# An encoder layer on one core: input also loaded by columns, and the latents turned behind the first Fourier product

## The chip, the core and the metric

The kernel runs on one core of a Trainium2 chip. The core has a matrix engine (TensorE, PE in the profile, with its weight loads as PEld), a vector engine (VectorE, DVE), an activation engine (ScalarE, ACT), a general engine (GpSimd, POOL) and a queue engine (SyncE, SP) that mostly issues DMA transfers. POOL can issue transfers too. Each engine works through its instructions in a fixed order and waits on semaphores for the others. [...]

The metric is the time of one execution on the device in microseconds (us), the median of several runs.

## The reference, cut to what matters

Two sequences of 1024 rows and 1024 columns go through one layer. Both changed stages lie at its start: the normalised and modulated input `h`, its projection to the latents (`q_lat`, `kv_lat`, `k_pe`), and the Fourier mixing of the remaining columns.

```python
def layer(x, c, ...):
    mod = jax.nn.silu(c) @ w_ada + b_ada
    sh1, sc1, ga1, sh2, sc2, ga2 = [m[:, None, :] for m in jnp.split(mod, N_MOD, axis=-1)]
    h = rmsnorm(x, g_mix) * (1.0 + sc1) + sh1
    z = h @ w_in
    q_lat, kv_lat, k_pe, f_in = z[..., :o1], z[..., o1:o2], z[..., o2:o3], z[..., o3:]
    y_mla = mla_group(q_lat, kv_lat, k_pe, g_q_lat, w_uq, g_kv_lat, w_ukv)
    y_four = fourier_group(f_in, w_four)      # 2-D Fourier transform, real part, by groups
    mix = jnp.concatenate([y_mla, y_four], axis=-1) @ w_out
    x = x + ga1 * mix
    h2 = rmsnorm(x, g_ffn) * (1.0 + sc2) + sh2
    ffn = (jax.nn.silu(h2 @ w_gate) * (h2 @ w_up)) @ w_down
    return x + ga2 * ffn
```

`rmsnorm` scales each row by the inverse root of its mean square. After the layer comes a last `rmsnorm`. All is float32.

## The kernel before, in words

Products of float32 are made from two halves: `split` puts a rounded high part (`hh`, `eoh`, `lh`, `wz_h`, ...) on ScalarE and the rest (`hl`, `eol`, `ll`, `wz_l`, ...) on VectorE (line 62 and 63), and `mm3` multiplies high with high, high with low and low with high (lines 78 to 80).

The first stage works on eight **pairs**, numbered 0 to 7: four for each sequence, each of two tiles of 128 rows. For pair k:

- `x_load(k)` loads the two row tiles `xt` (512 KB each; lines 353 to 356), from a ring of four buffers, two pairs' worth.
- `norm(k)` takes their mean squares on ScalarE (line 366), turns them into the row factors `rs_r` in six small steps on POOL (`rstd`, lines 103 to 110) and scales the rows on VectorE (line 369).
- `flip(k, g)`, for g from 0 to 3, transposes two of the eight column blocks of both tiles on TensorE (line 382: 4 transposes of 128x128, 16 in a pair), modulates them on ScalarE out of PSUM into `hf` (line 389) and splits `hf` into `hh` and `hl`. `hf` has one buffer, `hh` and `hl` two.
- `evenodd(k, i)` adds (i = 0) or subtracts (i = 1) the two tiles on POOL (line 400) and splits the result into `eoh`, `eol`.
- `zproj(k, u)` is the projection to the latents for tile u, 24 matmuls with 448 columns. Behind it come the mean squares of the latents on ScalarE (lines 413, 414), `rstd` on POOL, the scaling into `lat` on VectorE (lines 425, 426) and the store of the keys, `ckv_d`.
- `latents(k, u)` transposes `lat` on TensorE (line 440, four transposes) and splits and stores it (`lat_d`).
- `fourier_in(k, i)` is the Fourier product of the sum or the difference, 24 matmuls with 280 or 256 columns.

`pair(k)` puts these in order: TensorE does the projection of pair k and, between its products, the transposes of pair k+1, so that the next pair's `hh` is there when pair k ends. A generator (`extras`) is stepped between the products. In pair 0 it makes the eight products with folded output weights (`fold_out`, line 251; each leaves PSUM through VectorE into `so`, line 253, and is stored), in pairs 1 to 3 the eight chunks of a product with `w_ada` (line 216; 1 MB each, two buffers), in pairs 4 and 5 the products of line 311. `lat`, `so` and a few others share a ring of three buffers. Ahead of pair 0 stand the loads and products of the first modulation and the weights of the Fourier product.

The order on each engine is set when the program is built: the calls are laid out in the order of the code, shifted by a scheduler's estimate of when each can start. `behind()` and `tc.issue_after(...)` place work behind an instruction named before. A transfer waits in its queue until its buffer is free, and whatever stands behind it in that queue waits too.

Of the kernel before, what the change touches and what calls it, by code (L numbers as in the profile page):

```python
# [12 lines left out]
F32 = mybir.dt.float32  # L13
# [3 lines left out]
ALU = mybir.AluOpType  # L17
# [35 lines left out]
def hybrid_encoder_kernel(ctx: ExitStack, tc: tile.TileContext, a: dict):  # L53
# [109 lines left out]
    with ExitStack() as st:  # L163
# [5 lines left out]
        def bank():  # L169
            return pp.tile([P, 512], F32, tag="b", name="bank")  # L170

        def xtile():
            return w2.tile([P, D], F32, tag="x", name="xt", bufs=4)
# [178 lines left out]
        def x_load(k):  # L352
            s, j = pairs[k]
            st1["x", k] = [xtile() for _ in range(2)]
            for u in range(2):
                nc.sync.dma_start(st1["x", k][u], xs[s][rows(j, u), :])

        def norm(k):
            if ("x", k) not in st1:
                x_load(k)  # L360
            ms = tiny.tile([P, 2], F32, name="ms")
            xt = st1["x", k]
            for u in range(2):
                t = xt[u]
                jk = w.tile([P, D], BF16, tag="junk", name="junk", bufs=1)
                nc.scalar.activation(jk, t, AF.Square, scale=1.0 / 32.0, accum_out=ms[:, u : u + 1])
            r = rstd(ms, 2)
            for u in range(2):
                nc.vector.tensor_scalar(out=xt[u], in0=xt[u], scalar1=r[:, u : u + 1], scalar2=None, op0=ALU.mult)

        def flip(k, g):
            s, j = pairs[k]
            if g == 0:
                st1["hf", k] = w2.tile([P, NC, 2, P], F32, tag="hf", name="hf", bufs=1)
                st1["hh", k] = w.tile([P, NC, 2, P], F32R, tag=f"hh{k % 2}", name="hh")
                st1["hl", k] = w.tile([P, NC, 2, P], F32R, tag=f"hl{k % 2}", name="hl")
            hf, xt = st1["hf", k], st1["x", k]
            pt = bank().rearrange("p (c u t) -> p c u t", c=2, u=2)
            for c in range(2):
                for u in range(2):  # L380
                    cc = 2 * g + c
                    nc.tensor.transpose(pt[:, c, u, :], xt[u][:, cc * P : (cc + 1) * P], ident)
# [96 lines left out]
        def wide(tag, shape=(P, 4, 512)):  # L479
            return (w2 if tag == "hf" else w).tile(list(shape), F32, tag=tag, name="wide")  # L480
# [41 lines left out]
        x_load(1)  # L522
# [4 lines left out]
        wo2 = wo_load(0, wada_tile().rearrange("p a b -> p (a b)").rearrange("p (a b) -> p a b", a=2))  # L527
        mod_mm(0, 6, ch[6])
# [10 lines left out]
        with behind():  # L539
            fold_pe(wpe, gq)  # L540
        zproj(0, 0)
        norm(1)
        evenodd(0, 1)
        nk = len(pairs)
        more = extras()

        def pair(k, also=None):
            if k + 2 < nk:
                x_load(k + 2)
            if also is not None:  # L550
                also(0)
            if k > 0:
                zproj(k, 0)
# [22 lines left out]
            if k > 0:  # L576
                if k == nk - 1:
                    latents(k, 0)
                latents(k, 1)
# [4 lines left out]
            if k == 0:  # L584
                latents(k, 1)
# [3 lines left out]
        for k in range(nk - 1):  # L589
            pair(k)  # L590
# [1171 lines left out]
def _layout(i):  # L1762
# [10 lines left out]
    for s in range(2):  # L1773
# [4 lines left out]
        "x0": sq["x_prompt"][slots], "x1": sq["x_sample"][slots],  # L1778
        "cT": c.reshape(2, NC, P).transpose(2, 1, 0),
# [31 lines left out]
```

## Time and profile before

| | us |
|---|---|
| median of 3 runs | 2044.28 (2043.81 to 2044.97) |
| the profiled execution | 2045.76 |
| its span | 2043.9 |
| up to the end of pair 0's projections | 59.5 |
| from there to the first projection of pair 1 | 22.2 |
| pairs 1 to 6 | 131.7 |
| pair 7 | 17.6 |
| the rest of the layer | 1812.9 |

In the profile, a row of a timeline gives start, length, engine, line of the kernel, operation, output and inputs, and the number of instructions merged; in brackets stands the idle time of the engine before it and what ended it. A row of waits gives engine and line, what it waited for, the total in us, how often, and the longest. A row of groups gives busy us and mean ns of one, then the idle time before them. Matmuls overlap: their cost on the path is the distance from one start to the next, not their length.

### The profile page before, as it was taken

The numbers are of one execution on the slowest core, as the hardware profiler recorded it, in microseconds if no ns is written. First come the engines' busy times: TensorE is split into PE (matmuls) and PEld (weight loads), VectorE is DVE, ScalarE is ACT, GpSimd is POOL, SyncE is SP. The second block draws the span as 40 slices with busy tenths as digits, with TensorE's granted clock in tenths as the row PEclk, the third lists the DMA queues.
The fourth block names the chain that finished last, engine by engine and source line by source line (L and its number), as shares of the span: only waits on it lengthen the run. The fifth ranks groups of instructions, "written<-read, shape, count | busy, mean of one in ns | idle before, by whom it ended". The sixth has DMA issues, their size and how long they took to land.

```text
span 2043.9 us, 27849 instructions
## 1 busy us (share of the span) xinstructions
PE 1986.5 (97%) x9610; PEld 1613.6 (79%) x9610; DVE 1415.6 (69%) x2082; ACT 897.3 (44%) x1741; POOL 832.3 (41%) x1021
## 2 busy tenths in 40 slices
PE   6999999999999999999999999999999999999997
PEld 3788877888787777888888888877788888888876
DVE  3667757766677668878777676777766656667684
ACT  3656635555465554333333365453233333336451
POOL 0555213111313317879779410332654454420142
PEclk8999999999999999999999999999999999999999
DMA  9785694544644375546555587674333232258672
GB/s 363 229 258 180 220 336 132 129 104 106 158 114 129 119 277 192 195 157 210 194 166 196 173 306 251 216 233 140 129 118 103 97 110 103 96 187 276 226 228 89
DMA packets 183817, 370.30 MB, mean 181 GB/s; under 512 B 19004, under 2 KB 60476, under 8 KB 180604
## 3 DMA queue, kind: packets, MB, share of 16 engines
q1 hardware_dynamic: 165004, 310.72, 45.8%
q0 software_dynamic: 18672, 57.81, 9.5%
q8 instruction: 75, 1.23, 0.3%
q14 instruction: 66, 0.54, 0.1%
HBM read 256.46 MB, written 120.39 MB: 184 GB/s over the span
## 4 chain that ended last, share of the span: by engine, by line
PE 52%; DVE 3%; DMA 3%; POOL 1%; issue 1%; ACT 1%; SPq 0%; DVEq 0%; ACTq 0%; POOLq 0%
PE bank L78 17%; PE bank L79 17%; PE bank L80 17%; DVE wl L63 1%; DMA draw<-s_d 1%; ACT wh L62 1%; DMA val<-x_d 1%; DVE val L138 1%; POOL val L138 1%; DMA draw<-t_d 0%; DMA rgu<-in_wgu_dram 0%; DVE val L1610 0%; POOL rs_y L106 0%; DMA draw<-in_w_down_dram 0%; SPq L1570 0%
## 5 line engine op out<-in xcount | busy, mean ns | idle before, releaser
L78 PE MATMUL bank<-H,wh 128*128 128x512 f32 x1224 | 477.8, 390 | 6.9 <-DVE val L138 5.8
L80 PE MATMUL bank<-H,wl 128*128 128x512 f32 x1224 | 476.6, 390 | 0.2 <-DVE wl L63 0.2
L79 PE MATMUL bank<-H,wh 128*128 128x512 f32 x1224 | 476.3, 389 | 0.0
L138 DVE TENSOR_TENSOR val<-bank,val 128x512 f32<-128x512 f32 x244 | 166.7, 688 | 166.9 <-PE bank L80 165.8
L78 PEld LDWEIGHTS bank<-H,wh 128*128 128x128 f32 x1224 | 229.8, 188 | 59.0 <-DVE val L138 8.3
L80 PEld LDWEIGHTS bank<-H,wl 128*128 128x128 f32 x1224 | 229.8, 188 | 50.4 <-DVE wl L63 2.3
L79 PEld LDWEIGHTS bank<-H,wh 128*128 128x128 f32 x1224 | 229.8, 188 | 47.1
L63 DVE TENSOR_TENSOR wl<-draw,wh 128x512 fp32r<-128x512 f32 x286 | 202.2, 740 | 86.3 <-ACT wh L62 85.7
L62 ACT CAST wh<-draw 128x512 fp32r<-128x512 f32 x286 | 169.0, 620 | 158.6 <-PE bank L79 81.6
L79 PE MATMUL bank<-wl,wh 128*128 128x512 f32 x572 | 223.7, 391 | 2.8 <-DVE wl L63 2.8
L138 POOL TENSOR_TENSOR val<-val 128x512 f32<-128x512 f32 x58 | 83.4, 1445 | 343.4 <-DVE val L1584 189.6
L80 PE MATMUL bank<-wh,wl 128*128 128x512 f32 x572 | 222.7, 389 | 0.0
L78 PE MATMUL bank<-wh 128*128 128x512 f32 x572 | 222.6, 389 | 0.0
L62 ACT CAST wh<-rgu 128x512 fp32r<-128x512 f32 x171 | 106.3, 623 | 253.6 <-PE bank L79 192.1
L63 DVE TENSOR_TENSOR wl<-val,wh 128x512 fp32r<-128x512 f32 x133 | 139.7, 1052 | 68.8 <-ACT wh L62 68.7
L63 DVE TENSOR_TENSOR wl<-rgu,wh 128x512 fp32r<-128x512 f32 x171 | 169.1, 989 | 9.7 <-ACT wh L62 9.6
L62 ACT CAST wh<-val 128x512 fp32r<-128x512 f32 x133 | 82.3, 622 | 179.1 <-PE bank L79 156.5
L135 POOL TENSOR_TENSOR val<-rgu 128x512 f32<-128x512 f32 x80 | 114.8, 1435 | 99.2 <-DMA rgu<-in_wgu_dram 95.5
L79 PEld LDWEIGHTS bank<-wl,wh 128*128 128x128 f32 x572 | 107.4, 188 | 28.5 <-DVE wl L63 6.3
L78 PEld LDWEIGHTS bank<-wh 128*128 128x128 f32 x572 | 107.4, 188 | 22.5 <-ACT wh L62 0.2
L80 PEld LDWEIGHTS bank<-wh,wl 128*128 128x128 f32 x572 | 107.4, 188 | 21.9
L135 POOL TENSOR_TENSOR val<-val 128x512 f32<-128x512 f32 x89 | 119.3, 1357 | 1.3
(383 smaller groups left out, 3908.1 us busy)
## 6 DMA issues: line engine op xcount, KB each, us to landing
rgu<-in_wgu_dram SPq DMA_DIRECT2D x86, 512.0 KB
draw<-s_d SPq DMA_DIRECT2D x143, 256.0 KB
s_d<-val POOLq DMA_DIRECT2D x88, 256.0 KB, 3.8
draw<-t_d SPq DMA_DIRECT2D x88, 256.0 KB
s_d<-val SPq DMA_DIRECT2D x66, 256.0 KB
draw<-in_w_down_dram SPq DMA_DIRECT2D x55, 256.0 KB
wada<-in_w_ada_dram SPq DMA_DIRECT2D x13, 1024.0 KB
xt<-in_x_dram SPq DMA_DIRECT2D x16, 512.0 KB
```

What stands on the lines that cost most here:

```text
L62: here["a"] = nc.scalar.copy(hi, src).ins
L63: here["v"] = nc.vector.tensor_tensor(out=lo, in0=src, in1=rd(hi), op=ALU.subtract).ins
L78: nc.tensor.matmul(out, lh, rh, start=first, stop=False, skip_group_check=cont)
L79: nc.tensor.matmul(out, lh, rl, start=False, stop=False, skip_group_check=cont)
L80: nc.tensor.matmul(out, ll, rh, start=False, stop=last, skip_group_check=cont)
L135: return eng.tensor_tensor(out=out, in0=x, in1=y, op=ALU.subtract).ins
L138: return eng.tensor_tensor(out=out, in0=x, in1=y, op=ALU.add).ins
```

## The change

The input lies in DRAM a second time, turned by the host's layout: `xT0` and `xT1`, one block of 128x2048 for each pair, with the columns of x on the partitions. For pairs 1 to 7 the kernel loads this block straight into `hf` (`xT_load`), on SP's queue for pairs 1 and 2 and on POOL's queue for pairs 3 to 7. The transposes of x and the scaling of its rows are left out for these pairs. Since the row factors now run along the free dimension, two transposes turn them into PSUM (`scale_cols`), and two products on VectorE multiply `hf` by them in place; ScalarE modulates `hf` in place. The row tiles are still loaded, for their mean squares alone. `hf` has two buffers now and `xt` two instead of four.

The order is changed, too. `x_load(1)` and `xT_load(1)` come behind three weight loads, `norm(1)` ahead of pair 0's projections, pair 0 has an order of its own (`first_pair`), with its first Fourier product right behind its projections, and both latents of a pair are turned behind its first Fourier product.

```diff
         def xtile():
-            return w2.tile([P, D], F32, tag="x", name="xt", bufs=4)
+            return w2.tile([P, D], F32, tag="x", name="xt", bufs=2)
...
+        def xT_load(k):
+            s, j = pairs[k]
+            st1["hf", k] = w2.tile([P, NC, 2, P], F32, tag="hf", name="hf", bufs=2)
+            (nc.gpsimd if k > 2 else nc.sync).dma_start(st1["hf", k], a[f"xT{s}"][j])
...
             r = rstd(ms, 2)
+            if k > 0:
+                st1["r", k] = r
+                return
             for u in range(2):
                 nc.vector.tensor_scalar(out=xt[u], in0=xt[u], scalar1=r[:, u : u + 1], scalar2=None, op0=ALU.mult)
+
+        def scale_cols(k):
+            hf, r = st1["hf", k], st1.pop(("r", k))
+            pr = bank()[:, :256].rearrange("p (u t) -> p u t", u=2)
+            for u in range(2):
+                nc.tensor.transpose(pr[:, u, :], r[:, u : u + 1].broadcast_to([P, P]), ident)
+            for g in range(2):
+                gs = slice(4 * g, 4 * g + 4)
+                nc.vector.tensor_tensor(out=hf[:, gs], in0=hf[:, gs], in1=pr.unsqueeze(1).broadcast_to([P, 4, 2, P]), op=ALU.mult)
...
-            pt = bank().rearrange("p (c u t) -> p c u t", c=2, u=2)
-            for c in range(2):
-                for u in range(2):
-                    cc = 2 * g + c
-                    nc.tensor.transpose(pt[:, c, u, :], xt[u][:, cc * P : (cc + 1) * P], ident)
+            if k > 0:
+                pt = hf[:, 2 * g : 2 * g + 2]
+            else:
+                pt = bank().rearrange("p (c u t) -> p c u t", c=2, u=2)
+                for c in range(2):
+                    for u in range(2):
+                        cc = 2 * g + c
+                        nc.tensor.transpose(pt[:, c, u, :], xt[u][:, cc * P : (cc + 1) * P], ident)
...
-        x_load(1)
         wpe = w.tile([P, 2, HEADS * ROPE], F32, tag="lh", name="wpe", bufs=2)
...
         wo2 = wo_load(0, wada_tile().rearrange("p a b -> p (a b)").rearrange("p (a b) -> p a b", a=2))
+        x_load(1)
+        xT_load(1)
...
+        with behind():
+            norm(1)
+        placed = here["p"]
         zproj(0, 0)
-        norm(1)
-        evenodd(0, 1)
+        with tc.issue_after(placed):
+            evenodd(0, 1)
...
+        def first_pair():
+            x_load(2)
+            xT_load(2)
+            next(more)
+            zproj(0, 1)
+            fourier_in(0, 0)
+            scale_cols(1)
+            for g in range(4):
+                flip(1, g)
+            norm(2)
+            latents(0, 0)
+            for h in range(2):
+                fold_out(h, wo2, wuvT, gq)
+            next(more)
+            evenodd(1, 0)
+            next(more)
+            fourier_in(0, 1)
+            latents(0, 1)
+            evenodd(1, 1)
 
         def pair(k, also=None):
             if k + 2 < nk:
                 x_load(k + 2)
+                xT_load(k + 2)
...
-            if 0 < k < nk - 1:
+            if k < nk - 1:
+                scale_cols(k + 1)
                 flip(k + 1, 0)
                 flip(k + 1, 1)
             next(more, None)
             zproj(k, 1)
-            if k == 0:
-                fold_out(0, wo2, wuvT, gq)
-                flip(k + 1, 0)
-                flip(k + 1, 1)
-                fold_out(1, wo2, wuvT, gq)
-            if k < nk - 1:
-                latents(k, 0)
...
             fourier_in(k, 0)
-            if k > 0:
-                if k == nk - 1:
-                    latents(k, 0)
-                latents(k, 1)
+            latents(k, 0)
+            latents(k, 1)
...
-        for k in range(nk - 1):
+        first_pair()
+        for k in range(1, nk - 1):
             pair(k)
```

TensorE behind pair 0's second projection, before (`xt` is pair 1's x, `wuvT` the folded weights, `lat` pair 0's latents, `eoh` its sum of tiles):

```order
L80 MATMUL bank<-wz_h,hl 128x448
L251 MATMUL bank<-wada,wuvT 128x512 x2
L382 MATMUL bank<-ident,xt 128x128 x2
L251 MATMUL bank<-wada,wuvT 128x512
L382 MATMUL bank<-ident,xt 128x128 x6
L251 MATMUL bank<-wada,wuvT 128x512
L440 MATMUL bank<-ident,lat 128x128 x4
L382 MATMUL bank<-ident,xt 128x128 x8
L251 MATMUL bank<-wada,wuvT 128x512 x2
L78 MATMUL bank<-wcs_h,eoh 128x280
```

And now, from the end of the first Fourier product, which starts right behind the projections (`rs_r` holds pair 1's row factors):

```order
L80 MATMUL bank<-wcs_h,eol 128x280
L383 MATMUL bank<-ident,rs_r 128x128 x2
L461 MATMUL bank<-ident,lat 128x128 x4
L251 MATMUL bank<-wada,wuvT 128x512 x8
L78 MATMUL bank<-wcs_h,eoh 128x256
```

The 16 transposes of x are gone, and the latent's four now stand ahead of all eight folded products.

VectorE in the same place, before, from the last step of the key rotation of pair 0's second tile:

```order
L422 TENSOR_TENSOR t_562<-bank,ropes 128x32
L425 TENSOR_SCALAR lat<-bank,rs_r 128x256
L426 TENSOR_SCALAR lat<-bank,rs_r 128x128
L253 TENSOR_SCALAR so<-bank,gq 128x512
L63 TENSOR_TENSOR kv<-lat,kv 128x128
L369 TENSOR_SCALAR xt<-xt,rs_r 128x1024
L253 TENSOR_SCALAR so<-bank,gq 128x512
L63 TENSOR_TENSOR hl<-hf,hh 128x512
```

And now:

```order
L443 TENSOR_TENSOR t_564<-bank,ropes 128x32
L446 TENSOR_SCALAR lat<-bank,rs_r 128x256
L447 TENSOR_SCALAR lat<-bank,rs_r 128x128
L63 TENSOR_TENSOR kv<-lat,kv 128x128
L386 TENSOR_TENSOR hf<-hf,bank 128x1024 x2
L63 TENSOR_TENSOR ll<-bank,lh 128x512
L253 TENSOR_SCALAR so<-bank,gq 128x512
L63 TENSOR_TENSOR hl<-hf,hh 128x512
```

The two products that scale pair 1's columns stand behind the second latent, and the first eviction of a folded product behind them.

SP's queue around the loads of pair 1, before (`ckv_d` is the store of pair 0's keys):

```order
L356 DMA xt<-in_x_dram 128x1024 x2
L524 DMA wpe<-in_wpe_dram 128x512
L526 DMA wuvT<-in_wuvT_dram 128x512
L244 DMA wada<-in_w_out_dram 128x2x1024
L356 DMA xt<-in_x_dram 128x1024 x2
L244 DMA wada<-in_w_out_dram 128x2x1024
L260 DMA wq_d<-wq 128x1536
```

And now:

```order
L546 DMA wpe<-in_wpe_dram 128x512
L548 DMA wuvT<-in_wuvT_dram 128x512
L244 DMA wada<-in_w_out_dram 128x2x1024
L356 DMA xt<-in_x_dram 128x1024 x2
L361 DMA hf<-in_xT_dram 128x2048
L244 DMA wada<-in_w_out_dram 128x2x1024
L264 DMA w_1504<-in_w_dram 128x512
L356 DMA xt<-in_x_dram 128x1024
L260 DMA wq_d<-wq 128x1536
L356 DMA xt<-in_x_dram 128x1024
L452 DMA ckv_d_96<-kv 128x128
L452 DMA ckv_d_97<-kv 128x128
```

Pair 1's loads stand where pair 2's stood, and pair 2's two row tiles come one by one behind them.

More of the change, by code (lines that the diff above doesn't have):

```diff
@@ L479, in wide @@
         def wide(tag, shape=(P, 4, 512)):
-            return (w2 if tag == "hf" else w).tile(list(shape), F32, tag=tag, name="wide")
+            if tag == "hf":
+                return w2.tile(list(shape), F32, tag=tag, name="wide", bufs=2)
+            return w.tile(list(shape), F32, tag=tag, name="wide")
         cols0 = [(0, 2048)]
@@ L1778, in _layout @@
         "x0": sq["x_prompt"][slots], "x1": sq["x_sample"][slots],
+        **{f"xT{s}": x[slots].reshape(2, 4, P, NC, P).transpose(1, 4, 3, 0, 2)
+           for s, x in enumerate((sq["x_prompt"], sq["x_sample"]))},
         "cT": c.reshape(2, NC, P).transpose(2, 1, 0),
```

8 lines of the change are left out of this document (3 added, 5 removed).

## The prediction, made before the changed kernel was run

> **What bounds the kernel now.** I read the page's first part, then the span cut into stages, then TensorE's waits in the stage that the change touches, then the order of time there. (Columns of the stages: length, then busy us of each engine with its instructions, granted clock, share of the DMA engines, GB/s.)
>
> ```profile
> PE 1986.5 (97%) x9610; PEld 1613.6 (79%) x9610; DVE 1415.6 (69%) x2082; ACT 897.3 (44%) x1741; POOL 832.3 (41%) x1021
> ...
> 0.00:59.50 59.50, 40.27 (x213) 26.99 (x214) 28.11 (x67) 21.17 (x52) 9.65 (x20) 0.89 0.88 337
> 59.50:81.70 22.20, 17.74 (x89) 12.46 (x88) 14.66 (x30) 13.13 (x31) 13.72 (x32) 0.85 0.57 179
> 81.70:213.40 131.70, 130.45 (x842) 110.27 (x841) 88.17 (x184) 78.96 (x195) 68.15 (x149) 1.00 0.70 222
> 213.40:231.00 17.60, 16.66 (x107) 15.86 (x106) 12.10 (x29) 9.54 (x27) 7.14 (x18) 1.00 0.49 141
> 231.00:2043.90 1812.90, 1781.36 (x8368) 1448.00 (x8366) 1272.53 (x1775) 774.54 (x1439) 733.68 (x804) 1.00 0.54 174
> ```
> ```profile
> PE bank L382 <- DVE xt L369: 4.5, 1, 4.5
> PE bank L440 <- DVE lat L425: 2.2, 3, 0.9
> ```
>
> TensorE is the bound. The change touches the first two rows' end and the next two: 59.5 to 81.7 us is the first pair (weights' preparation before it), 81.7 to 213.4 are pairs 1 to 6, then pair 7. In pairs 1 to 6 TensorE is busy 130.45 of 131.70 us, so a TensorE instruction taken out there is worth its whole time. In the first pair it is idle 4.5 us. The order behind 231 us is the same in both kernels, row for row, so I move that stage as it is. The profiled execution took 2045.76 us, 1.86 around its span of 2043.9; the median of the three runs is 2044.28, 1.48 lower. I sum against the profile and take the difference over to the median.
>
> **The transposes taken out.** In a pair, 16 transposes of the next pair's x (L382) stand in two groups of 8:
>
> ```profile
> 86.55 1.03 PE L382 MATMUL bank<-ident,xt 128*128 128x128 f32 x8
> 87.52 1.06 PE L216 MATMUL bank<-wada,scT 128*32 128x512 f32 x8
> ...
> 93.45 0.60 PE L440 MATMUL bank<-ident,lat 128*128 128x128 f32 x4
> 93.89 1.04 PE L382 MATMUL bank<-ident,xt 128*128 128x128 f32 x8
> 94.86 1.06 PE L216 MATMUL bank<-wada,scT 128*32 128x512 f32 x8
> 95.85 0.39 PE L78 MATMUL bank<-wcs_h,eoh 128*128 128x280 f32 x1
> 99.06 0.60 PE L440 MATMUL bank<-ident,lat 128*128 128x128 f32 x4
> ```
> ```profile
> 206.18 1.04 PE L382 MATMUL bank<-ident,xt 128*128 128x128 f32 x8
> 206.97 0.38 PE L78 MATMUL bank<-wcs_h,eoh 128*128 128x280 f32 x1
> ```
>
> From start to next start a group takes 0.97 us ahead of other small work and 0.79 ahead of a long product. Of the twelve groups in pairs 1 to 6, eight are of the first kind and four of the second: 8 x 0.97 + 4 x 0.79 = 10.9 us. In their place come two transposes of the row scale in each pair. Four transposes take 0.44 (93.45 to 93.89), so two take about 0.25, 1.5 in six pairs. Net 9.4 us earlier. That is the firmest term.
>
> **What takes their place on the other engines.** VectorE loses two scalings of x (0.75 each) and gains two products of hf with a PSUM operand of 128x1024. The nearest rows are 128x512 with a PSUM operand: 0.68. Doubling gives at most 1.36, and one fixed part less gives some 1.23. So VectorE has about 1 us more in a pair, on 88.17/131.70, 67% busy; that hides behind TensorE. ScalarE runs the same eight activations, now from SBUF. No row shows one of 256 elements from SBUF. The nearest is the cast of twice as many, 0.63, so each lies between 0.32 and 0.63, against 0.58 now: -2.1 to +0.4 us in a pair, on an engine that is 60% busy. It is nearest to the activation itself, so I take no change.
>
> ```profile
> L315 DVE TENSOR_TENSOR so<-bank,gah 128x512 f32<-128x512 f32 x16 | 10.6, 681 | 0.0
> L369 DVE TENSOR_SCALAR xt<-xt,rs_r 128x1024 f32<-128x1024 f32 x10 | 7.1, 751 | 8.8 <-POOL rs_r L110 8.8
> L389 ACT ACTIVATE hf<-bank,sh,s 128x256 f32<-128x256 f32 x48 | 24.7, 576 | 0.0
> L62 ACT CAST hh<-hf 128x512 fp32r<-128x512 f32 x24 | 15.1, 630 | 0.2
> ```
>
> **The column loads.** Seven of 1 MB. The five on POOL's queue stand right behind the sums that free their buffer (hf has two), a whole pair and one projection ahead of their use, over 20 us. The nearest rows are transfers of 1 MB that POOL issues later in the kernel:
>
> ```profile
> L1096 POOL DMA_DIRECT2D hc_d<-hcb x4: 578/666/1003, 640.7 to 712.6; - x4
> ...
> DMA to landing us min/median/max: 8.3/8.9/11.1
> ```
>
> They land after 8.9 us, so the latency is covered twice over. The issue holds POOL for 0.67 us; behind it in POOL's row stand the next projection's statistics, which come some 5 us later. Pair 2's load is on SP's queue behind the key store of pair 0, issued near 67 us, and is needed past 84. Pair 1's x and columns are moved behind three weight loads on SP's queue, which come earlier by it and are waited for by nobody. What remains is the loads' share of the DMA engines: 0.5 us in the sum, between nothing and the 4.5 us of a rival below.
>
> **The first pair.** Here the order is rebuilt, so I follow the chain.
>
> ```profile
> 55.02 0.62 ACT L62 CAST eoh<-eo 128x512 fp32r<-128x512 f32 x1 [1.15 <-POOL eo L400]
> ...
> 58.37 1.05 ACT L366 ACTIVATE junk<-xt 128x1024 bf16<-128x1024 f32 x1
> ```
> ```profile
> 56.45 2.69 POOL L400 TENSOR_TENSOR eo<-hf 128x512 f32<-128x512 f32 x2 [1.46 <-DVE eol L63]
> ...
> 62.32 0.22 POOL L103 TENSOR_SCALAR rs_v<-ms 128x2 f32<-128x2 f32 x1
> ...
> 64.54 0.20 POOL L110 TENSOR_TENSOR rs_r<-rs_w,rs_y 128x2 f32<-128x2 f32 x1
> ```
> ```profile
> 59.33 1.88 PE L251 MATMUL bank<-wada,wuvT 128*128 128x512 f32 x4
> 65.67 0.66 PE L382 MATMUL bank<-ident,xt 128*128 128x128 f32 x2 [4.46 <-DVE xt L369]
> ```
> ```profile
> 71.94 1.88 PE L251 MATMUL bank<-wada,wuvT 128*128 128x512 f32 x4
> 73.25 0.69 PE L78 MATMUL bank<-wcs_h,eoh 128*128 128x280 f32 x1
> ...
> 81.66 0.45 PE L78 MATMUL bank<-wz_h,hh 128*128 128x448 f32 x1
> ```
> ```profile
> 47.34 0.81 SPq L356 DMA_DIRECT2D xt<-in_x_dram  x2
> ```
> ```profile
> 81.50 0.75 DVE L253 TENSOR_SCALAR so<-bank,gq 128x512 f32<-128x512 f32 x1 [1.70 <-DMA wo_d<-so]
> ```
>
> With two x buffers, pair 1's x can be issued only when pair 0's transposes end, where pair 2's is now (47.3); 8.9 us would put it at 56.2, just when ScalarE comes to it (55.6). TensorE reaches 59.33 as now and goes straight into the Fourier product (3.2 us, 95.85 to 99.06): 62.5. That covers the 4.46. But then it needs the first latent. Pair 1's two squares (1.05 each) now stand ahead of pair 0's on ScalarE, so pair 1's statistics reach POOL at 57.8 and take 2.4 there (62.32 to 64.74), to 60.2; behind them the two sums (2.7) and the statistics of pair 0's latent (2.4, with 0.6 for its key part) end near 65.9, and VectorE's scaling of the latent at 66.6. TensorE has 62.8 to 66.6 idle: the wait has moved, not gone. Behind it, the second latent's statistics hold VectorE's row until 71.2, because the products of hf stand behind that latent; they end at 73.6. The eight weight products (sixteen instructions in the trace, of which four take 1.31, 71.94 to 73.25: 5.2 in all) fill the free banks and wait for VectorE's evictions, the last three behind that point and on stores (the 1.70 row). Pair 1's projection starts near 79.7 in place of 81.66: 2.0 earlier. Bounds: with no wait at all 59.33 + 3.2 + 0.25 + 0.44 + 5.2 + 3.0 + 0.4 = 71.8, 9.8 earlier; with x landing late, 2 us later than now. I take 2.0, since each wait in it has a row.
>
> The granted clock shows what such a gap does:
>
> ```profile
> 65.00:70.00 5.00, 4.33 (x12) 2.71 (x13) 3.21 (x9) 2.07 (x6) 4.26 (x12) 0.50 0.20 52
> ```
>
> After the 4.46 us gap the clock was 0.50. The Trainium skill (TensorE: Matmul & The Clock Gate, Part 1) says an idle window of about 3.4 us halves the clock until a window of like length has been busy; the row agrees, and by that rule the gap of 3.8 us would cost up to 1.7 us more, a sum of 6.3 instead of 8.0 (an estimate from the page). I leave it out of the sum, as the slowed products would only wait for banks anyway.
>
> **The latents behind the first Fourier product.** Pair 7 already has that order:
>
> ```profile
> 226.12 0.60 PE L440 MATMUL bank<-ident,lat 128*128 128x128 f32 x4
> 227.66 0.63 PE L440 MATMUL bank<-ident,lat 128*128 128x128 f32 x4 [0.94 <-DVE lat L425]
> ```
>
> There the second latent comes 0.94 us after the 3.2 + 0.44 that cover it: its chain is 4.6 us. In pairs 2 and 3 a chunk of w_ada (0.97) covers it all but 0.3 each; pairs 4 and 5 have more cover; pair 6 has none (1.1): 1.7. Gone is the wait ahead of the first latent, 2.2 - 0.94 = 1.25. In pair 1 the chain is longer: the activations stand ahead of the squares on ScalarE and wait for pair 2's product on VectorE, which stands behind the last eviction and its store. I take 2.5 us, between 0 and the 4.5 of the first pair's wait.
>
> **Sum.** 2.0 + 9.4 + 1.25 - 1.7 - 2.5 - 0.5 = 8.0 us: 2037.8 for a profiled execution, 2036.3 for the median.
>
> **Rivals.** (a) The first pair's chain hides: evictions and statistics keep up, most of 9.8 us is won and pair 1's 2.5 isn't paid. 8.0 + 5 + 2 gives 2029.3. For it: VectorE is busy only 14.66 of 22.20 there; against it: the rows stand in a fixed order.
>
> (b) The column loads starve the chunks of w_ada.
>
> ```profile
> 75.00:90.00 15.00, 15.00 (x94) 12.57 (x93) 9.45 (x18) 6.42 (x16) 5.72 (x11) 1.00 0.94 297
> 90.00:105.00 15.00, 15.00 (x107) 12.62 (x106) 9.35 (x21) 9.37 (x22) 6.89 (x18) 1.00 0.92 285
> ```
>
> From 75 to 105 us the DMA engines are 93% busy at 291 GB/s, 313 if full: 1 MB costs 3.3 us. About 2.1 us are spare, and two loads want 6.7. If TensorE waits for the 4.5 us that are over, in place of the 0.5 in the sum, the time is 2040.3. Against it: no wait for w_ada stands in the stage now, and the chunks are asked for early. The Trainium skill (DMA: Bandwidth & Descriptors, Issuing engines are not separate DMA queues) says that transfers of all queues run on the same 16 engines, so POOL's queue would buy no bandwidth; no run yet shows it here.
>
> (c) Slower: the second latent's chain. Mean cover in pairs 1 to 6 is 4.8 us; each microsecond by which the chain is longer costs six. The sum holds 4.2 us of it. From a chain of 7.5 us on the kernel is slower by over 4.1; at 8 us it ends at 6 x 3.2 = 19.2 in place of 4.2, 2051.3. For it: VectorE and ScalarE do more between the squares and the latent than in pair 7; against it: 4.6 us is measured.
>
> **How the numbers follow.** Forecast 2036.3 (2033 to 2040) 0.53, (a) 0.16, (b) 0.22, (c) 0.09. A change under 0.2%, 4.1 us, can hardly be told from none. Faster: 0.50 of the forecast's, all of (a), 0.08 of (b): 0.74. Same: 0.03 and 0.13 of (b): 0.16. Slower: (c) and 0.01: 0.10. The range 2029 to 2045 leaves out (c) and the best half of (a).
>
> **What would show it.** Right: six stretches of a pair each shorter by about 1.6 us with TensorE still full; a wait of 3 to 4 us ahead of the first latent in place of the one ahead of L382; waits of about 1 us ahead of the second latent in pairs 1 and 6. Wrong: waits of L216 for w_ada between 85 and 120 us (b), waits for the second latent over 2 us in every pair (c), pair 1's projection before 76 us (a).

## The result, and the profile after

The change makes the kernel slower: 2052.99 us (median of 5 runs, 2051.64 to 2055.1) against 2044.28, a ratio of 1.0046 (95% interval 1.0035 to 1.0058). The forecast was 2036.3. The profiled execution took 2055.1 us, its span 2053.2.

The span after, cut at the same places as before: the first pair, pairs 1 to 6, pair 7, the rest.

```profile
60.50:78.70 18.20, 15.00 (x76) 9.76 (x74) 12.02 (x23) 11.96 (x27) 10.62 (x26) 1.00 0.61 201
78.70:224.50 145.80, 132.03 (x757) 105.91 (x758) 100.56 (x192) 81.27 (x196) 76.24 (x158) 0.94 0.77 251
224.50:241.30 16.80, 16.64 (x106) 15.84 (x106) 10.64 (x27) 9.65 (x27) 5.02 (x17) 1.00 0.41 120
241.30:2053.20 1811.90, 1779.60 (x8368) 1446.58 (x8366) 1271.92 (x1775) 774.37 (x1439) 733.66 (x804) 1.00 0.54 174
```

All of the loss is in pairs 1 to 6: 145.8 us in place of 131.7, with TensorE idle for 13.8 of them and its clock at 0.94. The waits of TensorE from the first pair to pair 7:

```profile
PE bank L216 <- DMA wada<-in_w_ada_dram: 7.8, 4, 6.3
PE bank L461 <- DVE lat L446: 7.5, 5, 2.4
PE bank L461 <- POOL lat L445: 0.6, 1, 0.6
```

Before, no wait for `w_ada` stood in this stage. By pairs, from first projection to first projection, the loss has two places, pair 1 (+9.3 us) and pair 6 (+6.5):

| | pair 1 starts at | pair 1 | pair 2 | 3 | 4 | 5 | 6 | 7 |
|---|---|---|---|---|---|---|---|---|
| before | 81.66 | 21.86 | 21.78 | 20.59 | 26.50 | 22.29 | 18.74 | 17.55 |
| after | 78.67 | 31.12 | 22.30 | 20.65 | 25.58 | 20.90 | 25.27 | 16.77 |

**Pair 1.** TensorE has done five of 24 matmuls of the first Fourier product when it comes to the second chunk of `w_ada` (columns of a row: start, length, engine, line, operation, and in brackets the idle time before it):

```profile
90.29 0.29 PE L79 MATMUL bank<-wcs_l,eoh 128*128 128x280 f32 x1
96.83 1.92 PE L216 MATMUL bank<-wada,scT 128*32 128x512 f32 x4 [6.26 <-DMA wada<-in_w_ada_dram]
```

SP's queue after, at that time, and its row for the same chunk before:

```profile
85.22 0.52 SPq L466 DMA_DIRECT2D lat_d<-lh  x1
85.79 1.31 SPq L466 DMA_DIRECT2D lat_d<-ll  x1
87.20 1.04 SPq L254 DMA_DIRECT2D wo_d<-so  x1
88.29 0.48 SPq L356 DMA_DIRECT2D xt<-in_x_dram  x1
88.86 0.44 SPq L207 DMA_DIRECT2D wada<-in_w_ada_dram  x1
89.42 1.15 SPq L452 DMA_DIRECT2D ckv_d<-kv  x2
92.67 1.46 SPq L207 DMA_DIRECT2D wada<-in_w_ada_dram  x3
```
```profile
86.10 1.49 SPq L207 DMA_DIRECT2D wada<-in_w_ada_dram  x2
```

A chunk is two transfers. Before, both were asked for from 86.10 on and used at 94.86. After, the first half is asked for at 88.86, behind stores of `so` and `lat`, the second at 92.67, behind the key store, and TensorE wants them at 90.4: it comes 4.4 us earlier than before, the requests 2.8 and some 6 us later. The DMA engines are full at that time, and the clock falls behind the gap:

```profile
90.00:95.00 5.00, 0.58 (x5) 0.35 (x3) 2.65 (x6) 5.00 (x14) 2.81 (x6) 0.98 1.05 373
95.00:100.00 5.00, 3.17 (x9) 1.50 (x10) 2.54 (x4) 1.93 (x5) 3.70 (x10) 0.50 0.95 370
100.00:105.00 5.00, 5.00 (x29) 3.67 (x30) 0.97 (x3) 0.64 (x2) 0.00 (x0) 0.84 0.02 6
```

**Pair 6.** The latents come late. The rows, of VectorE, POOL, ScalarE and TensorE in turn:

```profile
207.75 0.69 DVE L315 TENSOR_TENSOR so<-bank,gah 128x512 f32<-128x512 f32 x1 [1.56 <-DMA wm_d<-so]
208.35 1.21 DVE L386 TENSOR_TENSOR hf<-hf,bank 128x1024 f32<-128x1024 f32 x1
...
213.24 0.90 DVE L63 TENSOR_TENSOR hl<-hf,hh 128x512 fp32r<-128x512 f32 x1 [0.81 <-ACT hh L62]
...
214.19 0.47 DVE L446 TENSOR_SCALAR lat<-bank,rs_r 128x256 f32<-128x256 f32 x1
...
217.03 0.48 DVE L446 TENSOR_SCALAR lat<-bank,rs_r 128x256 f32<-128x256 f32 x1 [0.72 <-POOL rs_r L110]
```
```profile
207.96 0.20 POOL L110 TENSOR_TENSOR rs_r<-rs_w,rs_y 128x2 f32<-128x2 f32 x1
```
```profile
209.60 1.59 ACT L410 ACTIVATE hf<-hf,sh,s 128x256 f32<-128x256 f32 x3 [4.03 <-DVE hf L386]
...
213.11 0.38 ACT L434 ACTIVATE junk<-bank 128x256 bf16<-128x256 f32 x1
```
```profile
204.03 0.38 PE L383 MATMUL bank<-ident,rs_r 128*128 128x128 f32 x2
...
214.71 1.39 PE L461 MATMUL bank<-ident,lat 128*128 128x128 f32 x4 [2.39 <-DVE lat L446]
217.57 0.69 PE L461 MATMUL bank<-ident,lat 128*128 128x128 f32 x2 [1.48 <-DVE lat L446]
...
219.31 0.47 PE L461 MATMUL bank<-ident,lat 128*128 128x128 f32 x1 [0.63 <-POOL lat L445]
```

The row factors of pair 7 are in PSUM (the memory that TensorE's products go to) at 204.4, but the product of `hf` (L386) starts at 208.35: evictions of pair 5 into `so`, and two splits of `eo`, stand ahead of it on VectorE, and the last eviction waits 1.56 us for a buffer that a store still reads. ScalarE waits 4.03 us for that product with its activations (L410). Both latents are late by it. The first one's row factors are done at 208.2, but its scaling (L446, 214.19) stands on VectorE behind two splits of the new `hf`, which come behind the activations; TensorE waits 2.39 us for it. The squares of the second latent (L434) stand behind the activations themselves: 213.11, though the projection had ended at 209.2. The last part of that latent is turned at 219.31, ten us after its projection; in pair 7 of before the second latent was turned after 4.6. The clock halves, and from the last turned part to the next pair TensorE needs 5.2 us, where the whole second Fourier product of pair 6 took 2.9 before:

```profile
215.00:220.00 5.00, 2.89 (x11) 1.82 (x10) 3.64 (x9) 3.28 (x9) 4.01 (x10) 0.50 0.14 39
220.00:225.00 5.00, 5.00 (x25) 4.97 (x25) 1.89 (x3) 1.23 (x4) 2.56 (x2) 0.55 0.82 220
```

### The profile page after: what moved, and what is told of

It is laid out like the page before. It is cut to its first block, busy times and chain, and to the rows that moved or that the text cites. A ratio compares the mean times of both kernels' runs of the same rounds, so it can differ in the third digit from the quotient of the medians.

```text
span 2053.2 us, 27666 instructions
## 1 busy us (share of the span) xinstructions
PE 1985.6 (97%) x9512; PEld 1605.5 (78%) x9512; DVE 1420.9 (69%) x2082; ACT 899.0 (44%) x1741; POOL 834.7 (41%) x1026
## 3 DMA queue, kind: packets, MB, share of 16 engines
q8 instruction: 74, 1.21, 0.2%
## 4 chain that ended last, share of the span: by engine, by line
PE 53%; DMA 2%; DVE 2%; POOL 1%; issue 1%; ACT 1%; SPq 0%; DVEq 0%; ACTq 0%; POOLq 0%
PE bank L79 18%; PE bank L78 18%; PE bank L80 18%; DMA val<-x_d 1%; DVE wl L63 1%; DMA draw<-t_d 1%; POOL val L138 1%; DVE val L138 0%; ACT wh L62 0%; DMA draw<-s_d 0%; DVE val L1648 0%; DMA draw<-in_w_down_dram 0%; POOL rs_y L106 0%; DMA rgu<-in_wgu_dram 0%; SPq L1607 0%
```

## Experiments

Each kernel was run beside the kernel before, on the same chip. Executions of one kernel spread by up to 7 us around their median (the kernel before: 2039.92 to 2049.21 in 25 of them), and the part behind pair 7 alone took 1807 to 1816 us in the profiled ones. So the verdicts are the ratios to the runs of before, with their intervals, and the stages (one profiled execution each, in us) show where the time went in that execution. In runs with an early product, its two transposes count to the pair before. Remarks behind `#` in the excerpts of code were added for this text.

| | ratio to before (95%) | pair 1 starts | pair 1 | 2+3 | 4+5 | 6 | 7 |
|---|---|---|---|---|---|---|---|
| before | 1 | 81.66 | 21.86 | 42.37 | 48.79 | 18.74 | 17.55 |
| after | 1.0046 (1.0035-1.0058) | 78.67 | 31.12 | 42.95 | 46.48 | 25.27 | 16.77 |
| e4_old_order | 0.9999 (0.9990-1.0008) | 76.26 | 28.02 | 43.60 | 44.68 | 18.87 | 17.40 |
| e2_lat_first | 1.0012 (1.0003-1.0022) | 80.42 | 30.00 | 42.73 | 45.85 | 23.19 | 16.77 |
| e9_lat_only | 1.0002 (0.9991-1.0014) | 81.36 | 21.87 | 42.40 | 48.78 | 19.34 | 18.29 |
| e3_no_load | 1.0015 (1.0004-1.0025) | 79.10 | 27.61 | 40.05 | 45.85 | 24.86 | 16.79 |
| e5_chunk1 | 1.0023 (1.0013-1.0032) | 78.77 | 26.37 | 43.95 | 46.07 | 25.15 | 16.84 |
| e13_after_both | 1.0000 (0.9989-1.0011) | 78.60 | 24.43 | 40.12 | 45.57 | 24.67 | 16.78 |
| e1_ring4 | 1.0058 (1.0043-1.0073) | 78.97 | 32.61 | 45.26 | 46.96 | 21.11 | 16.89 |
| e6_early_product | 1.0039 (1.0025-1.0053) | 79.30 | 30.42 | 43.72 | 47.93 | 20.43 | 16.78 |
| e14_late_ring4 | 1.0044 (1.0031-1.0058) | 77.73 | 27.03 | 48.00 | 50.31 | 18.52 | 17.90 |
| e7_old_chunk1 | 0.9988 (0.9978-0.9999) | 76.67 | 24.80 | 43.48 | 44.66 | 18.84 | 17.31 |
| e8_old_both | 0.9967 (0.9954-0.9980) | 76.83 | 25.25 | 44.12 | 46.80 | 17.34 | 17.60 |
| e10_chunk1_pool | 0.9978 (0.9968-0.9988) | 78.02 | 23.28 | 40.95 | 47.49 | 20.50 | 17.36 |
| e11_late_load | 0.9981 (0.9972-0.9991) | 76.62 | 24.14 | 40.20 | 46.99 | 23.02 | 16.77 |
| e12_all | 0.9992 (0.9982-1.0003) | 78.91 | 24.24 | 40.14 | 53.80 | 17.90 | 17.21 |

### Which part of the change costs: the loads alone, and the two orders

**e4_old_order**: the column loads with the order of before.

```diff
-        first_pair()
-        for k in range(1, nk - 1):
+        for k in range(nk - 1):        # pair(0), norm(1), evenodd(0, 1) as before the change
...
             zproj(k, 1)
+            if k < nk - 1:
+                latents(k, 0)
...
             fourier_in(k, 0)
-            latents(k, 0)
-            latents(k, 1)
+            if k == nk - 1:
+                latents(k, 0)
+            if k > 0:
+                latents(k, 1)
```

> The column loads alone: xT into hf with two buffers, xt with two, the two products of hf, no transposes of x in pairs 1 to 7; but the order of before: pair 0 as before, the first latent behind the second projection. If the change of order is the cause of the loss, this is faster than before by most of the 9.4 us of transposes: 2035 to 2038. If the loads' share of the DMA engines is the cause (rival b), the waits for w_ada in pairs 1 to 3 stay at 8 to 10 us, and it ends at 2043 to 2046.

**e2_lat_first**: the changed kernel, with the first latent of pairs 1 to 6 turned right behind the second projection again, as before the change; the changed kernel's first pair stays.

> The first latent of pairs 1 to 6 is turned right behind the second projection again, as before the change; all else as after. Theory A (the ring of three held by both latents) and theory B (the latent order) both say that the pair-6 loss goes: waits for latents in pairs 4 and 6 under 1 us each, pair 6 back to 19 to 21 us, 2047 to 2049. If the loss of pair 6 came from the product of hf in place on VectorE and from the activations ahead of the squares on ScalarE (theory C), the wait only moves ahead of the first latent, and pair 6 stays at 24 to 26 us: 2052. Pair 1 stays at about 31 us by all of them, as w_ada is not touched.

**e9_lat_only**: the kernel before, with the latents' order of the change alone.

```diff
-            if k < nk - 1:
+            if k == 0:
                 latents(k, 0)
...
             if k > 0:
-                if k == nk - 1:
-                    latents(k, 0)
+                latents(k, 0)
                 latents(k, 1)
```

> The kernel before, with one part of the change alone: both latents of pairs 1 to 6 turned behind the first Fourier product (no column loads, pair 0 as before). If the latents' place costs by itself, through the ring of three that they hold longer (the run with this part undone was 6 us faster than after), it shows here too: waits for latents of 3 us or more in pairs 4 and 6, 2047 to 2051. If it costs only together with the product of hf in place, which comes late on VectorE and holds up ScalarE ahead of the squares, then here the second latent waits about 1 us in pair 6 and less elsewhere, as the prediction had it, and the time is 2043 to 2046.

The loads alone are level with before (0.9999), and neither end that was expected came: pair 1 starts 5.4 us earlier, pairs 4 and 5 take 4.1 us less, and pair 1 gives 6.2 back, 4.5 of it as a wait for `w_ada`. The first pair's new order then costs some 0.1% (1.0012, an interval that overlaps that of e4): with it pair 1 starts at 80.4 in this execution, 78.7 in that of after, and not at 76.3. The latents' order costs another 0.34% on top of that, 7 us, of which the two profiled executions show 2.3 up to the end of pair 7; the one of e2 was the slowest of its ten (2053.70, median 2047.03). Without the loads the latents' order costs nothing that can be measured (1.0002). There TensorE waits for latents 3.4 us in all, in pairs 4, 6 and 7:

```profile
PE bank L440 <- DVE lat L425: 3.4, 3, 1.6
```

With the loads, undoing the latents' order (e2) took 2.1 us off pair 6, to 23.2: neither the 19 to 21 of theories A and B nor the 24 to 26 of theory C. The order is part of the cause there, not the whole.

### Pair 1: a full DMA, or a late request

**e3_no_load**: the five loads of pairs 3 to 7 left out; these pairs work on the columns of pairs 1 and 2.

```diff
         def xT_load(k):
             s, j = pairs[k]
+            if k > 2:
+                st1["hf", k] = kept[k % 2]
+                return
```

> The five column loads of pairs 3 to 7 are left out (5 MB): these pairs work on what stands in hf since pairs 1 and 2, so that their results are not the layer's. Bandwidth (rival b of the prediction): the waits for chunks of w_ada in pairs 1 to 3 (about 10 us in all, 6.3 of it in pair 1) fall under 1.5 us, pairs 1 to 3 end about 10 us earlier, 2042 to 2044. Queue order (the chunk is issued late on SP's queue, 88.9 and 92.7 us, behind stores of so that wait for VectorE, and lands 3 to 4 us later in any case): the wait in pair 1 stays at 4 to 6 us, pairs 2 and 3 lose their waits (3.7 us), 2047 to 2050.

**e5_chunk1**: the second chunk asked for as soon as its buffer has been read.

```diff
-            fold_out(3, wo2, wuvT, gq)
+            # both products, then the load, then evictions and stores
+            nxt = fold_out(3, wo2, wuvT, gq, lambda: mod_load(1, cols1, wada_tile()))
```

> As after the change, but the load of the second chunk of w_ada is issued as soon as the last fold_out products have read its buffer, ahead of the two last evictions into so and their stores on SP's queue (after: 88.9 and 92.7 us, behind them). Queue order: it is issued before 83 us and lands before TensorE wants it at 90.6; the wait of 6.3 us and the half clock behind it go, pair 1 falls from 31.1 to 22 to 24 us, 2044 to 2046. Bandwidth: 1 MB brought forward pushes back the rest of what is under way between 80 and 100 us, so that a wait of 3 us or more for this chunk or the next remains in pair 1, and the stretch stays above 27 us: 2049 or more. Pair 6 stays at 25 us by both.

Without the loads, the wait in pair 1 was 3.4 us in place of 6.3, and pairs 2 and 3 lost theirs. With the early request (79.7 and 84.8 us on SP's queue, still behind stores), its longest part was 1.8, and waits of 2.3 us in all stayed in pairs 2 and 3. Each took back part of the 9.3 us, 3.5 and 4.7; neither theory was right alone.

**e10_chunk1_pool**: on e4, the same request on POOL's queue. **e11_late_load**: besides, the column loads of pairs 3 to 7 are asked for 11 to 16 us later.

```diff
-            nxt = fold_out(..., lambda: mod_load(1, cols1, wada_tile()))
+            nxt = fold_out(..., lambda: mod_load(1, cols1, wada_tile(), nc.gpsimd))
...
                 norm(k + 2)
+                if k > 0:
+                    xT_load(k + 2)      # no longer at the start of pair(k)
...
+            if k > 2:
+                nc.gpsimd.tensor_copy(st1["hf", k][:, 0, 0, 0:2], st1["rz"])
```

> Column loads with the order of before, and the second chunk of w_ada loaded on POOL's queue as soon as its buffer is free (about 74 us), past the stores that hold SP's queue up to 82 us. Queue order: it lands by 86 us, ahead of its use at 88, and no wait for it is left; pair 1 takes 22 us or less (24.8 with the early load on SP's queue). 2036 to 2039. Bandwidth: the wait moves to the third chunk, and pair 1 stays at 24 us or more: 2040 to 2042.

> As the run before it, and the column loads of pairs 3 to 7 are asked for about 10 us later, behind the statistics of the pair's second projection (POOL writes two of the row factors into the buffer first, which the load then overwrites). That leaves the DMA engines to the chunks of w_ada from 80 to 90 us. Bandwidth: the waits for w_ada in pairs 1 to 3 fall by 2 us or more against the run before it. Queue order: no change. Risk: the load is now needed some 10 to 12 us after its issue, and lands after 9.5; a wait of VectorE's product for it would show behind each first projection.

The request stands on POOL's queue at 76 us, and 0.6 us of waiting for `w_ada` is left in e10's whole stage, in pair 2; in e11 none.

```profile
75.98 1.19 POOL L207 DMA_DIRECT2D wada<-in_w_ada_dram  x2
```
```profile
PE bank L468 <- DVE lat L453: 7.7, 7, 2.4
PE bank L390 <- POOL rs_r L110: 2.0, 1, 2.0
PE bank L468 <- POOL lat L452: 1.0, 1, 1.0
PE bank L216 <- DMA wada<-in_w_ada_dram: 0.6, 1, 0.6
```

So with all column loads where the change has them, and the order of before, asking in time was enough to end these waits. Pair 1 stayed at 23.3 us even so, above the 22 that was expected, with a wait of 2.3 us for a latent. The loads' later place brought nothing more that can be measured (0.9978 and 0.9981).

Two things were moved, the request's place in the code and its queue. e7, further below, has the early place on SP's queue. SP's rows of e4 and of e7 for the second chunk (in e7 its first half is the second of the merged two, at 75.57):

```profile
86.96 1.19 SPq L207 DMA_DIRECT2D wada<-in_w_ada_dram  x1
89.07 0.33 SPq L207 DMA_DIRECT2D wada<-in_w_ada_dram  x1
```
```profile
74.98 1.55 SPq L207 DMA_DIRECT2D wada<-in_w_ada_dram  x2
...
81.41 0.46 SPq L207 DMA_DIRECT2D wada<-in_w_ada_dram  x1
```

The early place brings the first half forward by 11 us and the second by 7.7; POOL's queue brings nothing more for the first half and 4.8 us for the second (76.63). The Trainium skill (DMA: Bandwidth & Descriptors, Issuing engines are not separate DMA queues) says that another issuing engine saves only the time to initiate a transfer, usually little. Here it saved 4.8 us on one transfer, the time that this one stood behind two stores on SP's queue. That the engines behind the queues are shared, as the page also says, no run here tests by itself.

**e13_after_both**: both cures in the changed kernel, with its own order.

> The changed kernel with its own order, and both cures of w_ada at once: the second chunk on POOL's queue as soon as its buffer is free, and the column loads of pairs 3 to 7 asked for behind the second projection's statistics. If the late chunk is all that pair 1 lost, no wait for w_ada is left in pairs 1 to 3, pair 1 falls from 31.1 us to 22 or less and pairs 2 and 3 to 21 and 19.5; pair 6 keeps its 25 us: 2042 to 2044. If the latents behind the first Fourier product cost in pair 1 too, once the chunk no longer covers them, waits for latents of 2 us or more appear there, and pair 1 stays at 23 to 25 us: 2045 to 2047.

No wait for `w_ada` is left, pairs 1 to 3 take 64.6 us in place of 74.1, and the kernel is level with before: 2042.40 us, in the range of the first theory. But pair 1 stays at 24.4 us, as the second theory had it, for once the chunk is on time, the second latent is late:

```profile
94.15 0.60 PE L471 MATMUL bank<-ident,lat 128*128 128x128 f32 x4
98.47 0.70 PE L471 MATMUL bank<-ident,lat 128*128 128x128 f32 x4 [3.73 <-DVE lat L456]
99.10 1.06 PE L216 MATMUL bank<-wada,scT 128*32 128x512 f32 x8
```

### Pair 6: ring, order or product

**e1_ring4**: four buffers for `lat` and `so`. To make room, the squares of x are written over x, and the scratch tile `junk` is smaller.

```diff
-            return w.tile([P, 512], F32, tag="sk", name=name, bufs=3)
+            return w.tile([P, 512], F32, tag="sk", name=name, bufs=4)
...
-                jk = w.tile([P, D], BF16, tag="junk", name="junk", bufs=1)
+                jk = t if k > 0 else w.tile([P, D], F32, tag="eo", name="junk", bufs=1)
```

> The ring that lat, so, modrow and bga share gets four buffers instead of three. Theory A (the ring): pair 6 lost 6.5 us because both latents of a pair now hold two of three buffers up to the end of the first Fourier product, so the evictions of pair 5 into so waited for stores ahead of the product of hf on VectorE. With four buffers the waits for latents in pair 6 (4.5 us) and pair 4 (1.5 us) shrink to under 1.5 us together and the pair-6 stretch goes from 25.3 back to about 19 to 20 us: about 2046 to 2048. Theory B (the order itself: the second latent turned behind the first Fourier product comes late whatever the ring): the waits in pair 6 stay above 3 us, about 2052. On pair 1 (9.3 us lost, a wait of 6.3 us for the second chunk of w_ada): if late stores of so held up SP's queue, the chunk is issued 1 to 3 us earlier and the wait shrinks by as much; if it is the transfers' bandwidth, it stays at 6 us.

**e6_early_product**: the product of `hf` one projection earlier.

```diff
+            if k < nk - 1:
+                scale_cols(k + 1)
             zproj(k, 0)
...
-                scale_cols(k + 1)
                 flip(k + 1, 0)
```

> As after the change, but the two transposes of the row factors and the product of hf on VectorE for pair k+1 stand ahead of the first projection of pair k instead of behind it. Theory C (the product in place stands late on VectorE, behind evictions that wait for stores, so that the activations of hf hold up ScalarE ahead of the squares of the second latent): in pair 6 the waits for latents (4.5 us) fall under 1.5 us and the stretch goes from 25.3 to 19 to 21 us, in pair 4 the 1.5 us go, 2046 to 2048. If only the ring of three or the latents' order is to blame, pair 6 stays above 23 us: 2051 or more. Pair 1 isn't helped: its wait is for w_ada.

**e14_late_ring4**: e1's edit on e11.

> The order of before with column loads, the second chunk of w_ada on POOL's queue and the late column loads, and the ring of lat and so with four buffers in place of three. If the waits for latents that are left there (0.5 and 0.7 us in pair 4, 0.5 in pair 5, 2.6 and 0.6 in pair 6, with a half clock behind them) come from evictions into so that wait for their stores ahead of the product of hf, they fall to under 1.5 us in all, and pair 6 from 23.0 to under 20 us: 2035 to 2038. If the product and the activations behind it are late by themselves, pair 6 stays above 21 us, and the time at 2039 to 2042.

The fourth buffer took 4.2 us off pair 6 in e1 and 4.5 in e14 (23.0 to 18.5), as theory A expected, yet both kernels got slower. The room made for it is to blame, at least in part: with the squares of x no longer tied to one scratch tile, they moved ahead of the latents' squares on ScalarE in several pairs and wait there for x, 6.9 us in e1, 8.1 in e14, where e11 has 0.4 and after none.

```profile
ACT xt L380 <- DMA xt<-in_x_dram: 8.1, 4, 3.0
```

These two runs don't price the ring by itself. The early product took 2.0 us off pairs 5 and 6 together (44.2 in place of 46.2) and the wait out of pair 4: theory C holds in part. The time, 1.0039, can't be told from the change's 1.0046.

What differs throughout is how long VectorE's evictions in pairs 4 to 6 wait. The group of L315, 155 to 212 us, in before, e9, after, e13 and e11 (the last numbers are the idle time ahead of it):

```profile
L315 DVE TENSOR_TENSOR so<-bank,gah 128x512 f32<-128x512 f32 x16 | 10.6, 681 | 0.0
```
```profile
L315 DVE TENSOR_TENSOR so<-bank,gah 128x512 f32<-128x512 f32 x16 | 10.4, 680 | 0.0
```
```profile
L315 DVE TENSOR_TENSOR so<-bank,gah 128x512 f32<-128x512 f32 x16 | 10.5, 686 | 5.8 <-DMA wm_d<-so 2.6 <-DMA gah<-ga_d 2.5 <-DMA wn_d<-so 0.8
```
```profile
L322 DVE TENSOR_TENSOR so<-bank,gah 128x512 f32<-128x512 f32 x16 | 10.5, 683 | 6.4 <-DMA wm_d<-so 6.4
```
```profile
L322 DVE TENSOR_TENSOR so<-bank,gah 128x512 f32<-128x512 f32 x16 | 10.6, 682 | 4.8 <-DMA wm_d<-so 4.8
```

With column loads and latents behind the Fourier product the evictions wait 6 us, 2.5 of them in after for a load of `gah` and not for a store. With the latents' order alone they wait 0 (e9). But the loads with the order of before don't have one price: 1.4 us in e7, 1.8 in e4, 3.2 in e10 and 4.8 in e11. So the runs don't show that the two parts cost only together.

Pair 6 itself goes with one distance in all eleven profiled executions that have the product in its place: from the transposes of pair 7's row factors to the start of the product.

| us from L383 to the product | pair 6 | runs |
|---|---|---|
| 1.2 to 1.4 | 18.5 to 18.9 | e14, e7, e4 |
| 2.7 to 3.2 | 20.5 to 23.2 | e1, e10, e2, e11 |
| 3.9 to 4.3 | 24.7 to 25.3 | e3, e5, e13, after |

(The numbers of the lines are those of after.) With three buffers, the four runs with the change's order of the latents have the longest distances, and the five with the order of before lie between 1.3 and 3.2 us. The fourth buffer shortened the distance from 4.3 to 2.7 (e1, the change's order) and from 3.2 to 1.2 us (e14, that of before). So the runs point to the late product, as theory C has it, and to the ring of three that both latents hold as one thing that makes it late, as theory A has it. Why the distance differs so much among the runs with the order of before stays open.

### Versions that were to beat both

**e7_old_chunk1**: e4 with e5's edit. **e8_old_both**: besides, e6's edit. **e12_all**: e11 with e6's edit in pairs 5 and 6 only.

> The column loads with the order of before (as in the run of that name), and the second chunk of w_ada loaded early as well. Queue order: pair 1 there took 28.0 us with a wait of 4.5 us and a half clock behind it; without them 21 to 22 us, so 2035 to 2037, faster than before by 0.3 to 0.45%. Bandwidth: pair 1 stays at 25 us or more, 2039 to 2042.

> The column loads with the order of before, the second chunk of w_ada early, and the row factors' transposes and the product of hf ahead of the projection of the pair before. By theory C the waits for latents in pair 6 (0.8 and 1.0 us there) go too, and pair 6 takes 17.5 us instead of 18.9: 1 to 2 us below the run without the early product, 2033 to 2036. If the product's place matters only with latents behind the first Fourier product, the two are level.

> As the run before it, and in pairs 5 and 6 the row factors' transposes and the product of hf stand ahead of the pair's first projection. In pair 6 the waits for latents (0.8 and 1.0 us, with the early load on SP's queue) go, and the stretch falls from 18.8 to 17.5 us: 1 to 2 us below the run before it.

e8 is the fastest, 2038.63 us, 0.9967 (0.9954 to 0.9980) of before, though not in its 2033 to 2036; e10 and e11, at 0.9978 and 0.9981, can't be told from it. e7 fell short of its 2035 to 2037 (2042.32): a wait of 2.7 us for the next chunk remained in pair 1. e12 can't be told from before: pair 6 fell to 17.9 as expected, but pair 5 rose to 28.0: there the activations of `hf` came ahead of the first latent's squares, behind evictions that waited 2.3 us for a store, and TensorE waited 4.4 us for that latent.

## Why the prediction was wrong, point by point

- **The transposes out, net 9.4 us ("the firmest term").** The size was right where a pair is undisturbed: pair 5 fell by 1.39 us, and in e4 by 1.5 (20.77 against 22.29), 1.57 being the term's share. The two transposes of the factors step 0.14 us ahead of a long product (183.12 to 183.26), where 0.25 was taken.

```profile
183.12 0.38 PE L383 MATMUL bank<-ident,rs_r 128*128 128x128 f32 x2
183.26 0.45 PE L78 MATMUL bank<-wz_h,hh 128*128 128x448 f32 x1
```

- **The first pair, 2.0.** It won 3.0 (78.67 against 81.66). The wait moved ahead of the first latent, as said, but was 1.99 us and not 3.8, and the clock stayed at 1.00. What was missed: the loads with the old order win 5.4, so the new order lost 2.4 of them. The wait was 1.8 us shorter than taken and the term only 1.0 larger, so something else in it was too small; the near hit is in part luck.
- **The loads' share, 0.5; rival (b), 0.22.** This step failed. "The chunks are asked for early" held before (8.8 us ahead of use) and not after (1.5 us, the second half 2.3 us late): what is won ahead of a chunk takes from its lead, while its request stays tied to SP's queue, behind stores of `so` that VectorE sets free. The place was rival (b)'s, its mechanism only in part: without the five loads the wait in pair 1 fell from 6.3 to 3.4 us (e3), but with the order of before an earlier request cured it with every load in place (e10). In the changed order no run has the earlier request on POOL's queue alone; e13 has the later loads with it. The size was pairs 1 to 3 together, 9.5 us (74.1 to 64.6 in e13), half clock included, against 0.5 in the sum and 4.5 in the rival.
- **Pair 1's longer latent chain, 2.5.** 3.7 in e13, where the chunk no longer covers it. The mechanism was right, the term 1.2 too small.
- **The second latent, 1.7; the first one's wait gone, 1.25.** Without the loads the sum holds, 1.8 us against 1.7, though not its split: 0.9 us in pair 4 and 0.9 in pair 6 (e9), none in pairs 2 and 3. No wait is left ahead of the first latent. With the loads, pair 4 waits 1.5 and pair 6 4.5, and the clock halves. What failed is "VectorE has about 1 us more in a pair ... that hides behind TensorE": its share of busy time said nothing of its order. The product (1.21 us, as estimated) stands behind evictions, evictions behind stores, the activations behind the product, and behind the activations the second latent's squares and the splits that hold up the first latent. This was named for pair 1, and not carried over to pairs 4 to 6. Rival (c) gave a chain of 8 us in every pair; it was ten in one.
- **The range and the chances.** (b) and (c) were taken as alternatives. They came together; the range, which held (b) and left out (c), ended at 2045.
- **The rest of the layer** took 1811.9 against 1812.9, as assumed. By stages the sum is -3.0 + 9.3 + 0.6 - 2.3 + 6.5 - 0.8 = +10.3 up to the end of pair 7, and 1.0 back: 9.3, the difference of the spans.

## What to carry to other kernels

Time won on the bound engine shortens the lead of every transfer that is asked for at a fixed place in a queue: for each load behind the gain, set the time of its request against the new time of its use, and see what stands ahead of it in its queue. A queue that carries stores holds up the loads behind them; a load that is needed soon belongs ahead of the evictions, or on another queue. An instruction added to an engine that is 67% busy costs by what it stands behind and by what stands behind it: follow that order down to the next thing that the bound engine waits for, in every stage where the engine has evictions to make.

## What the runs showed of the hardware

- **The clock.** The length of a gap alone did not decide whether it halves. In pair 6 of after four transposes of the latent took 1.39 us behind a gap of 2.39, against 0.60 at full clock; the granted clock had been 1.00 up to 214 us. Behind a gap of 3.73 in pair 1 of e13 they took 0.70, and the clock stayed at 1.00:

```profile
95.00:100.00 5.00, 1.53 (x12) 0.56 (x12) 3.18 (x11) 4.54 (x14) 3.04 (x10) 1.00 0.85 293
100.00:105.00 5.00, 5.00 (x38) 4.79 (x35) 3.81 (x7) 2.16 (x5) 4.44 (x8) 1.00 0.93 282
```

The Trainium skill (TensorE: Matmul & The Clock Gate, Part 1) says that the window of about 3.4 us runs freely, so that the point of change varies; a gap of 3.73 that halves nothing agrees with that, one of 2.39 that does is shorter than the page has it, and the measurement decides.

- **A full DMA is not one rate.** At a share of 0.98 and 1.01 the engines moved 267 and 415 GB/s in two stretches of after, so 1 MB would cost 2.5 to 3.9 us (an estimate: 1.05 MB by those rates); the prediction's 313 GB/s was one point of that:

```profile
75.00:80.00 5.00, 4.62 (x36) 4.34 (x35) 4.26 (x7) 4.61 (x11) 2.34 (x2) 1.00 0.98 267
...
115.00:120.00 5.00, 5.00 (x28) 3.92 (x29) 3.70 (x9) 3.55 (x11) 2.27 (x8) 1.00 1.01 415
```
